# Two-layer hybrid encoder in exact-split fp32: rotary product and k's remainder from GpSimd to VectorE, softmax scaling from VectorE to ScalarE, three banks of transposes per head, and the per-layer input products inside the mixers

## Chip, cores and metric

One core of one Trainium2 chip. The metric is the device time of one launch in microseconds (us), the median of the runs. The five engines are named as the profile names them: PE is TensorE (PEld its weight loads), DVE VectorE, ACT ScalarE, POOL GpSimd, SP SyncE, which here only issues DMAs.

## What is computed

A residual stream h of 512 positions by 1024 features goes through two layers, in fp32:

```python
h = h + 0.5 * swiglu(rmsnorm(h, norm_ffn1[i]), ffn1_w_gate[i], ffn1_w_up[i], ffn1_w_down[i])
hn = rmsnorm(h, norm_mix[i])
if i % 2 == 0:
    h = h + ab_mixer(hn, w_in_ab[j], sink_a[j], w_out_ab[j], pos)
else:
    h = h + c_mixer(hn, w_in_c[j], rpb_c[j], w_out_c[j])
h = h + 0.5 * swiglu(rmsnorm(h, norm_ffn2[i]), ffn2_w_gate[i], ffn2_w_up[i], ffn2_w_down[i])
gate = jax.nn.sigmoid(rmsnorm(h, norm_ple[i]) @ w_ple_gate[i])
h = h + gate * (p[i] @ w_ple_proj[i])
```

and a last rmsnorm. The inner width of swiglu is 2816, p[i] has 256 features. The even layer's mixer has two parts on one projection. Part A is banded attention of 12 query heads on 4 key heads (|i-j| <= 128, rotary, a sink logit per head). Part B is dilated attention of 4 slots in three groups (offsets up to 64, 4 x 64 and 16 x 64), whose outputs are merged by their softmax denominators. The odd layer's mixer (part C below) is 16 heads of 8 x 16 neighbourhood attention with a position bias.

## The kernel before

**Layout.** Activations are held feature by position: eight chunks of 128 features by 512 positions. A product in full fp32 precision is made of three fp32r matmuls: each weight and each activation is split into a rounded part and the remainder (`split`, lines 120 to 122: ACT writes `hi`, another engine writes `lo = src - hi`), and `mm3` (lines 139 to 144) adds hi·hi, hi·lo and lo·hi. Weights come in units of 128 x 1024 (`unit`, line 129): SP issues the load, ACT makes `wh` (L121), DVE or POOL makes `wl` (L122). Three raw, four `wh` and four `wl` buffers are in turn. A wide matmul has 512 moving columns; the v projection (`project_v`, L322 to L324) has 256.

**Stages.** `setup`, then per layer `ffn`, `ab` or `c`, `ffn`, `ple`. In the trace `ab` is 376 to 660 us, `c` 1465 to 1700, the two `ple` about 1050 to 1106 and 2064 to 2125.

**Norm.** The norm's gain goes into the activation's split (`norm_split`); its factor per position comes late: `stat` (L187 to L190) makes `rcol`, one column per block of 128 positions, and `spread` transposes it into R, a row per position (property `R`, L206 and L214), by which products are scaled after the matmul.

**The AB mixer.** `ab` makes a list `steps` (scores and softmax, then p·v, head by head, from `a_steps` and `b_steps`) and a list `fill` (projections of q, k and v, then the first output products); `weave` (line 503) puts fill between steps by weights and by what a step needs. The order of each engine's own queue is then fixed by a scheduler before the run; `high_priority` marks pull some instructions ahead. Each engine runs its queue in order.

- `rope` (line 394) rotates a projected chunk: DVE shuffles (L404) and multiplies by the cosine (L405) out of PSUM, POOL multiplies by the sine (L406), DVE adds (L409, or L412 and L415 in another order of positions). It runs 20 times, 8 of them for part A.
- `stack_q` and `stack_k` (lines 262 to 285) write the rounded half and the remainder of a chunk. For k the remainder is made by POOL (L283), 8 times in `ab` and 16 times in `c`, and a DMA (L282) copies the rounded half to the other 64 partitions.
- `a_soft` (line 559), for each of 12 heads: four score blocks of 256 or 384 keys (`scores`, L428 on PE, L429 on DVE), ACT takes the exponentials with their sums (L568), DVE inverts the sums (L570) and scales the four blocks (L572).
- `windows_pv` (line 362) takes, for each of four key blocks, the two or three query blocks that see it, transposes them into one PSUM bank (`transposed`, L349), splits the bank on ACT and DVE (L121, L122) and multiplies by v (`pv`, L359 and L360). A's 12 heads and B's four slots do this: 16 times four banks.
- `b_steps`: `soft` for two slots, then `merge` (line 611), a chain of small DVE instructions (L617 to L634) that ends in the scaling of the blocks (L638), then `pv_r` (transposes L647, products L653) and `pv_n`.

**ple.** For each of eight output chunks, 24 wide matmuls of the gate and 6 of the product of p with `plp`, then DVE, ACT, DVE, DVE: the scaling by R, the sigmoid, the product, the sum. The last chunk of the last layer is done in two halves of positions. The two chunks of p are loaded and split at the stage's start.

## Time and profile before

| | us |
|---|---|
| runs: median of 3 (lowest to highest) | 2126.72 (2126.21 to 2127.21) |
| the profiled execution's own time | 2126.64 |
| its span in the trace | 2124.8 |
| PE busy in the span | 2085.4 |
| DVE busy | 1132.3 |
| ACT busy | 783.8 |
| POOL busy | 352.3 |

Read it so: PE is busy for all but 39.4 us of the span, so the other engines count only where PE stands idle for them, or where its clock is lowered. In the 40 slices of the page PE shows a digit under 9 only in the first and the last slice; the mixers' waits are too short for that view and are read from the waits of PE and from finer windows. Matmul ends are modelled, so a busy PE is not a PE at its peak.

### The profile page before, as it was taken

The page shows a single profiled execution, that of the slowest core. Times are in us where ns is not written, and L with a number is a line of the kernel's source. Part 1 is how long each engine was busy: PE and PEld are TensorE (multiplying, and loading weights), DVE is VectorE, ACT ScalarE, POOL GpSimd, SP SyncE. Part 2 cuts the span into 40 slices and gives each one's busy share as a digit, 9 for nine tenths or more (in the row PEclk, how much of TensorE's full clock was granted, in tenths as well). Part 3 has the DMA queues.
Part 4 walks back from the last instruction along what each step waited for, and adds up shares of the span by engine and source line. Part 5 has one row for each costly group of instructions (what it writes and reads, how often), then busy time and mean ns, then how long its engine had stood idle before and what let it go on. Part 6 is the DMA issues. An engine that isn't in the chain of part 4 may idle for free.

```text
span 2124.8 us, 25520 instructions
## 1 busy us (share of the span) xinstructions
PE 2085.4 (98%) x9950; PEld 1734.6 (82%) x9950; DVE 1132.3 (53%) x1793; ACT 783.8 (37%) x1255; POOL 352.3 (17%) x248
## 2 busy tenths in 40 slices
PE   8999999999999999999999999999999999999998
PEld 6888888777787888888888888888888888888886
DVE  6554432699786444543354555333778744553334
ACT  4332222465544333222343233223656533232232
POOL 3111101233211111101111111013222210110111
PEclk9999999999999999999999999999999999999999
DMA  5333333221223233333333322334333223323331
GB/s 171 98 99 99 95 96 98 85 75 56 65 68 92 90 99 99 99 90 96 105 97 99 99 93 93 95 97 124 105 105 102 82 90 99 99 91 96 94 107 60
DMA packets 75385, 202.02 MB, mean 95 GB/s; under 512 B 16896, under 2 KB 24576, under 8 KB 75264
## 3 DMA queue, kind: packets, MB, share of 16 engines
q1 hardware_dynamic: 74976, 200.29, 30.8%
q8 instruction: 78, 1.28, 0.3%
q14 instruction: 43, 0.35, 0.1%
q10 hardware_dynamic: 288, 0.10, 0.0%
HBM read 191.97 MB, written 2.59 MB: 92 GB/s over the span
## 4 chain that ended last, share of the span: by engine, by line
PE 89%; DVE 5%; ACT 2%; issue 1%; POOL 1%; DMA 0%; SPq 0%; DVEq 0%; POOLq 0%; ACTq 0%
PE mm L143 15%; PE mm L144 15%; PE mm L142 15%; PE sc L142 12%; PE sc L143 12%; PE sc L144 12%; PE mm L322 1%; PE mm L323 1%; PE mm L324 1%; PE tr L349 1%; PE ob L359 1%; PE ob L360 1%; PE sc L428 1%; ACT wh L121 1%; DVE act L572 1%
## 5 line engine op out<-in xcount | busy, mean ns | idle before, releaser
L121 ACT ACTIVATE wh<-wr 128x1024 fp32r<-128x1024 f32 (+1 forms) x360 | 374.6, 1042 | 995.0 <-issue 431.1
L122 DVE TENSOR_TENSOR wl<-wr,wh 128x1024 fp32r<-128x1024 f32 (+1 forms) x343 | 510.2, 1488 | 314.1 <-ACT wh L121 313.1
L143 PE MATMUL mm<-act,wh 128*128 128x512 f32 (+1 forms) x1560 | 609.7, 391 | 3.0 <-DVE act L169 2.1
L142 PE MATMUL mm<-act,wh 128*128 128x512 f32 (+1 forms) x1560 | 609.1, 391 | 1.0 <-ACT wh L121 0.6
L144 PE MATMUL mm<-act,wl 128*128 128x512 f32 (+1 forms) x1560 | 608.3, 390 | 0.5 <-DVE wl L122 0.5
L144 PE MATMUL sc<-act,wl 128*128 128x512 f32 (+1 forms) x1138 | 442.5, 389 | 0.8 <-DVE wl L122 0.8
L142 PE MATMUL sc<-act,wh 128*128 128x512 f32 (+1 forms) x1138 | 442.9, 389 | 0.0
L143 PE MATMUL sc<-act,wh 128*128 128x512 f32 (+1 forms) x1138 | 442.5, 389 | 0.0
L143 PEld LDWEIGHTS mm<-act,wh 128*128 128x128 f32 x1560 | 293.4, 188 | 64.4 <-DVE act L169 5.3
L142 PEld LDWEIGHTS mm<-act,wh 128*128 128x128 f32 x1560 | 293.3, 188 | 60.0 <-ACT act L121 1.5
L144 PEld LDWEIGHTS mm<-act,wl 128*128 128x128 f32 x1560 | 293.2, 188 | 58.4 <-DVE wl L122 1.0
L239 POOL TENSOR_TENSOR tmp<-tmp,tmp 128x512 f32<-128x512 f32 x88 | 115.2, 1309 | 818.5 <-DVE tmp L238 783.7
L144 PEld LDWEIGHTS sc<-act,wl 128*128 128x128 f32 x1138 | 213.7, 188 | 45.1 <-DVE wl L122 1.2
L143 PEld LDWEIGHTS sc<-act,wh 128*128 128x128 f32 x1138 | 213.7, 188 | 44.1
L142 PEld LDWEIGHTS sc<-act,wh 128*128 128x128 f32 x1138 | 213.6, 188 | 43.8
L238 DVE TENSOR_TENSOR tmp<-sc,R 128x512 f32<-128x512 f32 x88 | 60.8, 691 | 276.8 <-PE sc L144 276.8
L180 POOL TENSOR_TENSOR ssq<-ssq,tmp 128x512 f32<-128x512 f32 x55 | 90.2, 1639 | 552.6 <-ACT tmp L175 525.7
L236 DVE TENSOR_TENSOR tmp<-mm,R 128x512 f32<-128x512 f32 x88 | 60.8, 691 | 130.4 <-PE mm L144 127.9
L121 ACT ACTIVATE act<-tmp 128x512 fp32r<-128x512 f32 x92 | 58.3, 634 | 117.3 <-POOL tmp L239 116.2
L322 PE MATMUL mm<-wh,act 128*128 128x256 f32 x256 | 74.4, 291 | 0.3 <-DVE act L337 0.3
L323 PE MATMUL mm<-wl,act 128*128 128x256 f32 x256 | 73.9, 289 | 0.0
L324 PE MATMUL mm<-wh,act 128*128 128x256 f32 x256 | 73.8, 288 | 0.0
(142 smaller groups left out, 1621.8 us busy)
## 6 DMA issues: line engine op xcount, KB each, us to landing
wr<-in_gu_dram SPq DMA_DIRECT2D x176, 512.0 KB, 3.5
wr<-in_dn_dram SPq DMA_DIRECT2D x64, 512.0 KB, 3.5
wr<-in_dn_dram SPq DMA_DIRECT2D x32, 384.0 KB, 3.1
wr<-in_qk_ab_dram SPq DMA_DIRECT2D x20, 512.0 KB, 3.5
wr<-in_plg_dram SPq DMA_DIRECT2D x16, 512.0 KB, 3.5
wr<-in_qk_c_dram SPq DMA_DIRECT2D x16, 512.0 KB, 3.7
act<-act SPq DMA_DIRECT2D x40, 128.0 KB, 2.2
wr<-in_v_ab_dram SPq DMA_DIRECT2D x8, 512.0 KB, 3.8
```

Source lines behind the costliest of these rows:

```text
L121: self.nc.scalar.activation(hi, src, AF.Copy)
L122: (lo_eng or self.nc.vector).tensor_tensor(lo, src, hi.bitcast(F32), op=ALU.subtract)
L142: mm(out, stat[0], mov[0], start=start, stop=False)
L143: mm(out, stat[0], mov[1], start=False, stop=False)
L144: mm(out, stat[1], mov[0], start=False, stop=stop)
L180: eng.tensor_tensor(self.acc, self.acc, sq, op=ALU.add)
L236: nc.vector.tensor_tensor(t1, pgu[0], R, op=ALU.mult)
L238: nc.vector.tensor_tensor(t2, pgu[1], R, op=ALU.mult)
L239: nc.gpsimd.tensor_tensor(t2, t1, t2, op=ALU.mult)
L322: nc.tensor.matmul(ps[b], xh, h, start=first, stop=False, skip_group_check=True)
L323: nc.tensor.matmul(ps[b], xh, l, start=False, stop=False, skip_group_check=True)
L324: nc.tensor.matmul(ps[b], xl, h, start=False, stop=last, skip_group_check=True)
```

## The change

- `rope`: the product with the sine (new L435) is made by VectorE.
- `stack_k`: k's remainder (new L287) is made by VectorE, in both mixers.
- `a_soft`: ScalarE scales the blocks (new L613).
- `windows_pv`: three groups of key blocks, (1), (2) and (0, 3), with 384, 384 and 512 columns, in place of four banks of 256, 384, 384 and 256. The 10 transposes and the 8 products per head stay.
- `ple_proj`: the products of p[i] with `plp` (8 chunks of 6 wide matmuls per layer) become fill steps of `ab` and of `c`. ACT copies each from PSUM (L417), SP stores it in DRAM (L418), and `ple` loads it again (L888). In `ab` two of them stand near the start, six at the end; in `c` they come after the projections.
- The start of `ab`: the first k and q are projected before R is spread (`first`), and the first v, the second v (`vb`) and the rest change places in `fill`.
- `act` has 60 buffers, 59 before; `identb`, which nothing reads, is gone; `idle` takes R's buffer.

```diff
@@ spread, R
+    def spread(self, rcol, late=False):
...
-            self.nc.tensor.transpose(rp[:, b * P:(b + 1) * P], rcol[:, b:b + 1].broadcast_to([P, P]), self.ident)
+            ins = self.nc.tensor.transpose(rp[:, b * P:(b + 1) * P], rcol[:, b:b + 1].broadcast_to([P, P]), self.ident)
+            if late and b == 0:
+                self.tc.keep_in_program_order(ins)
@@ stack_k
-            nc.gpsimd.tensor_tensor(low[hf][own, :], k[own, :], t[own, :].bitcast(F32), op=ALU.subtract)
+            nc.vector.tensor_tensor(low[hf][own, :], k[own, :], t[own, :].bitcast(F32), op=ALU.subtract)
@@ windows_pv
+    GROUPS = ((1,), (2,), (0, 3))
...
+        for g in self.GROUPS:
+            at = [(x, b) for x in g for b in range(*self.window(x))]
+            off = lambda x, b: (x - self.window(b)[0]) * P
+            parts = self.transposed([es[b][:, off(x, b):off(x, b) + P] for x, b in at])
+            n = 0
+            for x in g:
+                lo, hi = self.window(x)
+                m = n + (hi - lo) * P
+                self.pv(o[:, lo * P:hi * P], vcol(x), [y[:, n:m] for y in parts], g == (1,), x == 3)
+                n = m
@@ new
+    def ple_proj(self, i):
+        nc, io = self.nc, self.io
+        c = {"p": []}
+        for k in range(2):
+            raw = self.tmp()
+            nc.sync.dma_start(raw, io["pT"][i, :, k, :])
+            c["p"].append(self.split_chunk(raw, nc.vector))
+        def chunk(m):
+            if m % 4 == 0:
+                c["u"] = self.unit(io["plp"][i, m // 4])
+            s = m % 4 * 2 * P
+            b = self.sbank() if i == 0 and m < 2 else self.bank()
+            self.mm_unit(b, tuple(x[:, s:s + 2 * P] for x in c["u"]), c["p"], True, True)
+            t = self.tmp()
+            nc.scalar.activation(t, b, AF.Copy)
+            nc.sync.dma_start(self.pp[i, m], t)
+        return [(("pp", m), .25, lambda m=m: chunk(m)) for m in range(KC)]
@@ rope
-        nc.gpsimd.tensor_tensor(t2, t2, self.sinr, op=ALU.mult)
+        nc.vector.tensor_tensor(t2, t2, self.sinr, op=ALU.mult)
@@ ab
+        def first():
+            pk = self.project(w[12])
+            self.rcol
+            pq = self.project(w[13])
+            self.spread_R(late=True)
+            end_k(0, pk)
+            end_q(0, 0, pq)
...
-        fill = (a0[:2] + proj_v("va", 0) + a0[2:] + a1 + proj_b(0) + proj_v("vb", 1) + proj_v(("vr", 0), 2)
-                + proj_b(1) + proj_v(("vr", 1), 3))
+        b0, b1, pp = proj_b(0), proj_b(1), self.ple_proj(0)
+        fill = (a0[:1] + pp[:2] + proj_v("va", 0) + a0[1:] + proj_v("vb", 1) + a1 + b0
+                + proj_v(("vr", 0), 2) + b1 + proj_v(("vr", 1), 3) + pp[2:])
@@ a_soft
-            nc.vector.tensor_scalar_mul(es[b], es[b], rd[:, b:b + 1])
+            nc.scalar.activation(es[b], es[b], AF.Copy, scale=rd[:, b:b + 1])
@@ c
+        fill += self.ple_proj(1)
@@ ple
+            pm = self.tmp()
+            nc.sync.dma_start(pm, self.pp[i, m])
...
-                pg, pp = self.bank()[:, x], self.sbank()[:, x]
+                pg = (self.sbank() if m % 2 else self.bank())[:, x]
                 self.mm_unit(pg, u, cut(xg), True, True)
-                self.mm_unit(pp, upm, cut(p), True, True)
...
-                nc.vector.tensor_tensor(t2, pp, t1, op=ALU.mult)
+                nc.vector.tensor_tensor(t2, pm[:, x], t1, op=ALU.mult)
```

How this moves instructions, at three places. The number behind a tile's name tells one buffer of that name from another.

**The start of `ab`, on TensorE.** `mm_2622` (after: `mm_2603`) is the first q's projection, `tr_2589` (after: `tr_2629`) the transposes that spread R, `mm_2731` the first v's projection. Before:

```order
L142 MATMUL mm_2622<-act_2062,wh_2617 128x512
L143 MATMUL mm_2622<-act_2063,wh_2617 128x512
L144 MATMUL mm_2622<-act_2062,wl_2618 128x512
L206 MATMUL tr_2589<-ident,rcol_2586 128x128 x4
L142 MATMUL mm_2622<-act_2155,wh_2617 128x512
L143 MATMUL mm_2622<-act_2156,wh_2617 128x512
```

After:

```order
L141 MATMUL mm_2603<-act_2526,wh_2598 128x512
L142 MATMUL mm_2603<-act_2527,wh_2598 128x512
L143 MATMUL mm_2603<-act_2526,wl_2599 128x512
L206 MATMUL tr_2629<-ident,rcol_2594 128x128 x4
L326 MATMUL mm_2731<-wh_2734,act_1876 128x256
L327 MATMUL mm_2731<-wl_2735,act_1876 128x256
```

The four transposes stood behind 9 of the 24 matmuls of that projection and stand behind all 24 now. From them to the first scores there were 15 wide matmuls and 39 of 256 columns; now there are 95 of 256 columns.

**Part A's softmax.** The second head's scaling and the first head's split banks (`tmp<-tr`), before on VectorE:

```order
L122 TENSOR_TENSOR tmp_2900<-tr_2896,tmp_2899 128x256
L569 TENSOR_TENSOR st_a_2816<-st_a_2816 128x4
L409 TENSOR_TENSOR act_2886<-tmp_2881,tmp_2882 128x512
L570 RECIPROCAL st_a_2816<-st_a_2816 128x4
L122 TENSOR_TENSOR tmp_2910<-tr_2905,tmp_2909 128x384
L572 TENSOR_SCALAR act_2818<-act_2818,st_a_2816 128x256
L572 TENSOR_SCALAR act_2823<-act_2823,st_a_2816 128x384
L122 TENSOR_TENSOR tmp_2920<-tr_2915,tmp_2919 128x384
L572 TENSOR_SCALAR act_2828<-act_2828,st_a_2816 128x384
L122 TENSOR_TENSOR tmp_2929<-tr_2925,tmp_2928 128x256
L572 TENSOR_SCALAR act_2833<-act_2833,st_a_2816 128x256
```

After, on ScalarE (L609 is the exponential, L613 the scaling):

```order
L613 ACTIVATE act_2688<-act_2688,st_a_2671 128x256
L609 ACTIVATE act_2855,st_a_2853<-act_2855,st_a_2853 128x256
L120 ACTIVATE tmp_2937<-tr_2933 128x384
L607 ACTIVATE st_a_2853<-st_a_2853 128x4
L609 ACTIVATE act_2860,st_a_2853<-act_2860,st_a_2853 128x384
L120 ACTIVATE tmp_2947<-tr_2943 128x384
L609 ACTIVATE act_2865,st_a_2853<-act_2865,st_a_2853 128x384
L609 ACTIVATE act_2870,st_a_2853<-act_2870,st_a_2853 128x256
L120 ACTIVATE tmp_2958<-tr_2953 128x512
L613 ACTIVATE act_2855<-act_2855,st_a_2853 128x256
```

The scalings left VectorE's queue and stand in ScalarE's behind the next head's exponentials and the split of the bank before.

**The first merge of part B, on VectorE.** Before:

```order
L617 COPY s_b_4591<-st_b_4240 32x4 x16
L621 TENSOR_TENSOR zs_b_4610<-s_b_4591,st_b_4240 128x8
L622 TENSOR_TENSOR w_b_4608<-s_b_4591,zs_b_4610 128x2x4
L623 TENSOR_TENSOR w_b_4608<-st_b_4240,zs_b_4610 128x2x4
L625 TENSOR_TENSOR z_b_4609<-w_b_4608,s_b_4591 128x2x4
L626 TENSOR_TENSOR z_b_4609<-w_b_4608,st_b_4240 128x2x4
L627 TENSOR_TENSOR zs_b_4610<-z_b_4609 128x8
L628 RECIPROCAL zs_b_4610<-zs_b_4610 128x8
L629 TENSOR_TENSOR w_b_4608<-w_b_4608,zs_b_4610 128x2x4
L630 TENSOR_TENSOR w_b_4608<-w_b_4608,zs_b_4610 128x2x4
L634 COPY w_b_4621<-w_b_4608 32x2 x16
L638 TENSOR_SCALAR act_4263<-act_4263,w_b_4608 128x256
```

After, its first and its last rows (the copies are L658 and L675 now, the scaling L679):

```order
L433 STREAM_SHUFFLE tmp_4663<-mm_4637 128x512
L434 TENSOR_TENSOR tmp_4662<-mm_4637,act_2635 128x512
L658 COPY s_b_4568<-st_b_4339 32x4 x12
L435 TENSOR_TENSOR tmp_4663<-tmp_4663,act_2636 128x512
L658 COPY s_b_4568<-st_b_4339 32x4 x4
L662 TENSOR_TENSOR zs_b_4587<-s_b_4568,st_b_4339 128x8
L438 TENSOR_TENSOR act_4667<-tmp_4662,tmp_4663 128x512
```

```order
L675 COPY w_b_4598<-w_b_4585 32x2 x6
L433 STREAM_SHUFFLE tmp_4713<-mm_4687 128x512
L434 TENSOR_TENSOR tmp_4712<-mm_4687,act_2635 128x512
L675 COPY w_b_4598<-w_b_4585 32x2 x10
L679 TENSOR_SCALAR act_4362<-act_4362,w_b_4585 128x256
```

Six instructions of two rotations (L433, L434, L435, L438, L433, L434) stand inside the chain now; before there were none between its first copy and its first scaling. On TensorE, between the last score product ahead of this merge and the first transposition behind it, there were 29 matmuls of 256 columns and 25 wide ones, and there are 46 wide ones now. At the second merge there were 25 and 28, and there are 24 and 26; its chain on VectorE has no rotation in it, before or after.

## Rows read from the trace of the kernel before

**Rows 1.** The page's first part: an engine's busy time, its share of the span, its instructions.

```profile
PE 2085.4 (98%) x9950; PEld 1734.6 (82%) x9950; DVE 1132.3 (53%) x1793; ACT 783.8 (37%) x1255; POOL 352.3 (17%) x248
```

**Rows 2.** Busy time by stretch: start and end in us; its length; then, for PE, PEld, DVE, ACT and POOL, the busy us and the number of instructions; then the granted clock of PE, the DMA share and GB/s. The four stretches of `ab` (its start, part A, the first and the second half of part B), an `ffn`, and `c`.

```profile
376.00:397.00 21.00, 17.02 (x98) 14.86 (x97) 12.25 (x20) 5.27 (x8) 10.81 (x8) 0.95 0.39 124
397.00:545.00 148.00, 140.00 (x804) 118.24 (x803) 129.14 (x330) 87.82 (x212) 43.42 (x31) 1.00 0.20 61
545.00:600.00 55.00, 51.12 (x278) 42.09 (x277) 41.41 (x119) 25.23 (x61) 15.79 (x11) 0.91 0.21 63
600.00:660.00 60.00, 57.05 (x357) 47.45 (x356) 43.29 (x128) 27.25 (x67) 2.57 (x2) 1.00 0.16 54
660.00:1040.00 380.00, 380.00 (x1684) 314.77 (x1683) 175.97 (x169) 118.53 (x147) 51.67 (x35) 1.00 0.32 100
1465.00:1700.00 235.00, 230.27 (x1365) 200.36 (x1365) 169.09 (x447) 135.20 (x282) 63.13 (x42) 1.00 0.35 101
```

**Rows 3.** The waits of PE over the whole span: which instruction waited for which; us in total, times, longest. The row behind the dots is from the same view of part A alone (397 to 545 us), since it waits so in other stages too.

```profile
PE tr L349 <- DVE act L572: 5.1, 6, 1.6
PE tr L647 <- DVE act L638: 4.3, 2, 2.6
PE sc L428 <- DVE act L270: 2.5, 1, 2.5
PE tr L206 <- POOL rcol L190: 1.4, 1, 1.4
...
PE ob L360 <- DVE tmp L122: 2.4, 2, 1.6
```

**Rows 4.** Busy time by stretch, as in rows 2, for the three stretches of `ab` in which PE's granted clock was 0.50.

```profile
394.80:398.20 3.40, 2.93 (x11) 2.93 (x12) 2.28 (x7) 0.06 (x1) 0.00 (x0) 0.50 0.03 11
548.40:555.20 6.80, 6.24 (x25) 5.70 (x25) 3.71 (x15) 6.05 (x21) 0.00 (x0) 0.50 0.00 0
568.90:572.30 3.40, 2.94 (x8) 2.46 (x9) 3.37 (x8) 0.00 (x0) 1.89 (x3) 0.50 0.15 48
```

**Rows 5.** The chain that ended last, followed through the start of `ab`: start us, us, engine, tile and line.

```profile
380.53 2.39 POOL wl L122
...
383.96 0.67 PE tr L206 x4
...
384.65 0.61 ACT R L214
...
386.65 1.29 POOL tmp L406
...
391.78 1.78 DVE act L409
...
394.24 0.98 DVE act L270
395.23 0.04 issue
395.27 0.80 PE sc L428 x2
```

**Rows 6.** Groups of equal instructions of the AB mixer (376 to 660 us), shapes kept apart: line, engine, operation, tiles, shapes, count; busy us in all, mean ns of one; idle us before them and what ended it.

```profile
L406 POOL TENSOR_TENSOR tmp<-tmp,act 128x512 f32<-128x512 f32 x20 | 25.7, 1293 | 78.5 <-DVE tmp L404 65.2 <-PE mm L324 6.7 <-ACT wh L121 3.4
...
L572 DVE TENSOR_SCALAR act<-act,st_a 128x256 f32<-128x256 f32 x24 | 16.5, 687 | 0.2
...
L404 DVE STREAM_SHUFFLE tmp<-mm 128x512 f32<-128x512 f32 x20 | 15.0, 748 | 0.0
...
L283 POOL TENSOR_TENSOR act<-act,act 64x512 fp32r<-64x512 f32 x8 | 13.8, 1722 | 9.0 <-ACT act L281 8.8
L405 DVE TENSOR_TENSOR tmp<-mm,act 128x512 f32<-128x512 f32 x20 | 13.5, 676 | 0.1
...
L572 DVE TENSOR_SCALAR act<-act,st_a 128x384 f32<-128x384 f32 x24 | 9.4, 418 | 0.0
...
L331 ACT ACTIVATE act<-mm,rcol 128x256 f32<-128x256 f32 x8 | 3.2, 469 | 0.0
...
L401 DVE TENSOR_TENSOR act<-act,R 128x512 f32<-128x512 f32 x1 | 0.7, 684 | 0.0
```

**Rows 7.** VectorE and then POOL in order of time around 439 us: start us, us, engine, line, operation, tiles, shapes, count (equal ones merged), in brackets the idle time before. The last row is the view of L572 alone: shortest, median and longest of one in ns, the first's and last's start.

```profile
438.87 2.99 DVE L572 TENSOR_SCALAR act<-act,st_a 128x256 f32<-128x256 f32 x4
...
438.42 2.37 POOL L122 TENSOR_TENSOR wl<-wr,wh 128x1024 fp32r<-128x1024 f32 x1 [9.95 <-ACT wh L121]
...
L572 DVE TENSOR_SCALAR act<-act,st_a x48: 336/407/2480, 404.4 to 537.1; 128x256 f32<-128x256 f32 x24, 128x384 f32<-128x384 f32 x24
```

**Rows 8.** Two matmuls of the v projection that follow each other, in order of time.

```profile
388.73 0.28 PE L323 MATMUL mm<-wl,act 128*128 128x256 f32 x1
388.85 0.28 PE L324 MATMUL mm<-wh,act 128*128 128x256 f32 x1
```

**Rows 9.** Around the first merge, in order of time: TensorE behind the last score product and at the first transposition, then ScalarE, then VectorE.

```profile
557.30 0.39 PE L323 MATMUL mm<-wl,act 128*128 128x256 f32 x1
...
569.36 0.47 PE L647 MATMUL tr<-ident,act 128*128 128x128 f32 x1 [2.62 <-DVE act L638]
...
558.20 1.06 ACT L121 ACTIVATE wh<-wr 128x1024 fp32r<-128x1024 f32 x1 [3.25 <-PE mm L324]
...
559.79 4.63 DVE L617 COPY s_b<-st_b 32x4 f32<-32x4 f32 x16 [1.39 <-ACT act L608]
```

**Rows 10.** VectorE at the very end, in order of time: the last scalings by gain and norm.

```profile
2116.20 5.17 DVE L917 SCALAR_TENSOR_TENSOR act<-h,gain,tr 128x256 f32<-128x256 f32 x13
```

More of the change, by code (lines that the diff above doesn't have):

```diff
@@ L60, in __init__ @@
         self.open = {}
+        self.pp = self.dp.tile([DEPTH, KC, P, T], F32, name="pp")
     def nm(self, s):
@@ L104, in setup @@
         nc.scalar.activation(warm, self.ones[:, 0:1], AF.Silu)
-        idle = self.cp.tile([P, T], BF16, name="idle")
+        idle = self.small("R", [P, T], BF16, bufs=1)
         nc.vector.memset(idle, 0.0)
@@ L210, in R, with spread_R @@
     def R(self):
-        if self.rt is None:
-            self.rt = self.small("R", [P, T], bufs=1)
-            self.nc.scalar.activation(self.rt, self.spread(self.rcol), AF.Copy)
+        return self.rt or self.spread_R()
+    def spread_R(self, late=False):
+        self.rt = self.small("R", [P, T], bufs=1)
+        self.nc.scalar.activation(self.rt, self.spread(self.rcol, late), AF.Copy)
         return self.rt
@@ L459, in proj, with end_k, end_q @@
             return key, 1, lambda: t.__setitem__(key, self.rope(self.project(w[i]), kind))
-        def proj_a(gp):
-            def k_step():
-                k, low = self.rope(self.project(w[12 + 4 * gp]), "n"), self.lows()
-                t["ak", gp] = (self.stack_k(k, low), low)
-            def q_step(j):
-                t["aq", gp, j] = self.stack_q(self.rope(self.project(w[13 + 4 * gp + j]), "n"))
-            return [(("ak", gp), 1, k_step)] + [(("aq", gp, j), 1, lambda j=j: q_step(j)) for j in range(3)]
+        def end_k(gp, p):
+            k, low = self.rope(p, "n"), self.lows()
+            t["ak", gp] = (self.stack_k(k, low), low)
+        def end_q(gp, j, p):
+            t["aq", gp, j] = self.stack_q(self.rope(p, "n"))
+        def first():
[5 more added lines that the diff above has]
+            end_q(0, 0, pq)
+        def proj_a(gp):
+            out = [(("aq", gp, j), 1, lambda j=j: end_q(gp, j, self.project(w[13 + 4 * gp + j]))) for j in range(1 - gp, 3)]
+            k = ("ak", 1), 1, lambda: end_k(1, self.project(w[16]))
+            return [k, *out] if gp else [(("ak", 0), 2, first), *out]
         def proj_b(sp):
@@ L553, in a_steps @@
             if i < len(heads):
-                steps.append(([("ak", gp), ("aq", gp, heads[i][1])], 1, lambda h=heads[i]: soft(*h)))
+                need = [("ak", gp)] + [("aq", gp, heads[i][1])] * (gp + heads[i][1] > 0)
+                steps.append((need, 1, lambda h=heads[i]: soft(*h)))
             if i:
@@ L841, in ple @@
         nc, io = self.nc, self.io
-        xg, p = self.xg, []
-        for c in range(2):
-            raw = self.tmp()
-            nc.sync.dma_start(raw, io["pT"][i, :, c, :])
-            p.append(self.split_chunk(raw))
-        up, ends = None, []
+        xg, ends = self.xg, []
         for m in range(KC):
             u = self.unit(io["plg"][i, m])
-            if m % 4 == 0:
-                up = self.unit(io["plp"][i, m // 4])
-            s = m % 4 * 2 * P
-            upm = tuple(x[:, s:s + 2 * P] for x in up)
+            pm = self.tmp()
+            nc.sync.dma_start(pm, self.pp[i, m])
             half = k_next == N_NORM - 1 and m == KC - 1
```

13 lines of the change are left out of this document (1 added, 12 removed).

## The prediction, made before the changed kernel ran

> **What bounds the kernel now.** The page's first part comes first: PE is busy 2085.4 of a span of 2124.8 us [rows 1], so all that can be won is 39.4 us of idle PE and the stretches in which its clock is lowered. The profiled execution took 2126.64 us, 1.84 more than its span and 0.08 under the median of the runs, 2126.72. My sum is made against 2126.64. The table by stretch comes next: an `ffn` has no idle PE, and of the AB mixer its start has 4.0 us (21.00 less 17.02), part A 8.0, the two halves of part B 3.9 and 2.95, the mixer of the second layer 4.7 [rows 2]. The change touches the mixers and `ple` alone. The waits of PE then say whom these gaps wait for: VectorE's scaling in A (5.1), the merges (4.3), the first scores (2.5), R (1.4), and in A VectorE's split of a bank (2.4) [rows 3]. Last, the clock: the granted clock is 0.50 (1.2 GHz of 2.4) in three stretches around such gaps, with 2.93, 6.24 and 2.94 us of matmuls in them [rows 4]. Half of each, 1.5, 3.1 and 1.5 us, is what full clock would give back.
>
> TensorE's own work does not change. 48 wide matmuls per layer move from `ple` to the mixer, each 0.226 us (380.00 over 1684 [rows 2]); a v-projection matmul starts 0.12 us behind the last [rows 8]. A move in itself is worth nothing, except where a moved matmul stands where PE waited.
>
> **Start of `ab`: -4.9.** Before, R's transposes run at 383.96 after a wait of 1.4, R is written at 384.65, and the rotation and k's split end at 395.23, when PE has long run out [rows 3, 5]. In the changed order 15 more wide matmuls, 3.4 us, stand ahead of the transposes, more than the 1.4 waited: that wait goes. Behind them stand 95 half-width matmuls, 11.4 us. PE is free at 382.56 without its wait, begins R at 386.0, ends it (0.67) at 386.6 and arrives at the scores at 398.0. The chain: R to 387.3 (0.61), cosine and sine by R (2 x 0.68 [rows 6]), two rotations begun (0.68, 0.75, 0.68, 2 x 0.68, 0.69), a weight's split that waits for a free buffer and then takes 1.06 [rows 9] and a subtraction of two times 0.68, then the remainders, sum and copies: about 398.1. The two nearly meet, so 2.0 of the 2.5 goes, and with it the low-clock stretch, 1.5. Bounds: -5.4 if the whole wait goes, -1.4 if R's alone does.
>
> **Part A: -4.8.** Here the trace says why VectorE is late. The 128x256 scaling takes 687 ns on average, the wider 128x384 one 418 [rows 6]; four small ones take 2.99 us where POOL makes a `wl` of 2.37 at the same time, and of all 48 the shortest takes 336 and the longest 2480 [rows 7]. So one that meets POOL's subtraction stands still for it. On VectorE over the whole mixer: 20 sine products of two SBUF inputs at 0.684 (the row L401), +13.7; 8 remainders, +5.5; two `plp` units and two chunks of p split, +2.7 and +1.4; the scalings, -16.5 and -9.4 [rows 6]. That is 2.6 less in 284 us, and PE no longer waits for it between exponential and transpose. ScalarE gets 24 scalings at about 0.47 (L331, the same shape) and 24 at about 0.6, an estimate from it by the columns: some 25 us, so in A its 87.8 of 148 busy [rows 2] becomes some 113 of the 143 left, 79%. POOL loses 25.7 and 13.8. I take all of the 5.1, half of the 2.4, and give 1.5 back for heads whose scaling stands behind other work of ScalarE, since the first transposition now needs three scaled blocks, not two. Bounds: -7.5 (both waits gone) to +6.4 (a rival below).
>
> The three groups in place of four banks spare 16 instructions on each of ScalarE and VectorE. They have no price of their own here and lie under PE's work; counted at nothing.
>
> **First merge: +2.4.** The last score product starts at 557.30, the first transposition at 569.36 after a wait of 2.62, and the 16 small copies at 559.79 after 1.39 idle [rows 9]. Six instructions of rotations now stand inside this chain: 0.75 + 0.68 + 0.68 + 0.69 + 0.75 + 0.68, 4.2 us by the rows of L404, L405 and L401 [rows 6]. The first two fit in the 1.39 idle, so the chain grows from 12.1 to 14.9. PE's cover grows too, from 9.44 to 46 x 0.226 = 10.4. The wait becomes 4.5, +1.9, and I add 0.5 for a longer stretch at low clock. Bounds: 0 (the rotations are done before the chain can begin) to +4.8 (nothing fits in the idle time, +1.4, and one more stretch like the third of [rows 4], +1.5).
>
> **Second merge: +0.9.** Its chain stays; its cover falls by one half-width and two wide matmuls, 0.6 us, more if the low clock holds on: 0 to +2.
>
> **The mixer of the second layer: -0.6.** 16 remainders go from POOL, 1722 ns each [rows 6], to VectorE at 0.684, 11 us in a stage where VectorE is busy 169.09 of 235 [rows 2], and the 48 moved products give cover at its end. Bounds -2 to +2: its 4.7 us of gaps have many owners.
>
> **`ple` and the end: -0.7.** Each of the 16 chunks is now stored and loaded again. The load stands on SP behind the weights' loads; the work that hides it is 24 matmuls of the gate (5.4 us) and the sigmoid. If it is late, only the sum of h is late, and the other weights of the gate go on: counted at nothing within `ple`. At the very end six half-width matmuls (6 x 0.12) no longer stand between the last two halves; VectorE's 5.17 us of last scalings [rows 10] may hide them all, so -0.7 to 0.
>
> **Sum:** -4.9 - 4.8 + 2.4 + 0.9 - 0.6 - 0.7 = -7.7, so 2118.9. The longest low-clock stretch, in A's last heads (6.24 us), I leave as it is, since p·v and scores alternate there as before.
>
> **The rivals.** A measurement tells about 0.2%, 4.3 us, from no change: below 2122.4 is faster, above 2130.9 slower.
>
> *ScalarE becomes what A waits for: slower (0.10).* Each of 12 heads' scalings may stand behind one weight split, 1.06 [rows 9]: 12.7 in place of the waits, A +6.4. It decides once a head waits for over 0.6 us on average (that is 7.5 over 12). With the merge at its upper bound: -4.9 + 6.4 + 4.8 + 0.9 - 0.6 - 0.7 = +5.9, 2132.5. For it: the queue is in order and A is already ScalarE's fullest stretch of `ab`. Against: 79% is not full, and splits are made ahead of need.
>
> *VectorE is not relieved: no change (0.18).* In A the waits only change name (A 0), and the merge comes at its upper bound: -0.5, 2126.1. The rows allow it: undisturbed, the scalings cost 24 x 0.336 + 24 x 0.407 [rows 7], 17.9 us and not 25.9, against 23.3 us added. VectorE then has 5.4 us more to do, and if POOL's subtraction no longer meets anything it stops, nothing is won by moving. With the merge as forecast this gives -4.9 + 0 + 2.4 + 0.9 - 0.6 - 0.7 = -2.9, 2123.7; 0.08 of the 0.18 is this one. The Trainium skill, "VectorE: DVE Perf Modes", section "Mode 2×_2P — use both read ports for one tensor", speaks for it: a scaling of one fp32 tensor can use both read ports and make two results per cycle, while a product of two tensors cannot, so the change trades VectorE's cheap kind of work for its dear one. The trace agrees on the rates (from 336 ns, the shortest, which has 256 columns, to 407, about what 384 take, 128 columns cost 71 ns, while 512 columns of two tensors take 684); but the four scalings of 2.99 us show that the cheap rate was not had where it counted, and I follow them.
>
> *Relief carries through: faster by more (0.17).* The waits of A all go, the chain of the merge is reached early, and the low-clock stretch of A's last heads goes too: -5.4 - 7.5 + 0 - 3.1 + 0.9 - 0.6 - 0.7 = -16.4, 2110.2. Against: the rotations stand inside the chain by VectorE's order.
>
> That the moved products do not fill what waited is already in the sum: they get 0.6 at most.
>
> **How the numbers follow.** The forecast has 0.55; its own range is 2114 to 2124 (the bounds of start, A's share of 2.4 and merge taken together but not all at one end), 0.05 of it above 2122.4. Faster: 0.50 + 0.17 = 0.67. Same: 0.05 + 0.18, less 0.02 for its worst part: 0.21. Slower: 0.12. The range from 2110.0 to 2128.0 leaves out half of the larger gain (0.085) and the slower cases (0.11).
>
> **What would show it.** Start: no wait for `rcol`, a wait under 1 us for the first scores, full clock at 394.8. A: the waits of the transposes name ScalarE's scaling, and add up to under 3 us. Merge: a wait of about 4.5 before the first transposition and rotations between the small copies. End: less idle PE. I am wrong if the waits for scalings in A exceed 6 us, if the first merge waits for under 2.5 or over 6, or if a wait appears in `ple` for the loaded products.

## The result, and the profile after

The changed kernel takes 2130.26 us (median of 17 runs, 2127.36 to 2133.48) against 2126.22 of the kernel before in the same comparison: ratio 1.0019, 95% interval 1.0011 to 1.0026. That is 4 us slower, where 7.7 us faster were forecast. The profiled execution took 2133.08, 2.8 over its median, with a span of 2131.3, so the stretches below hold some 2.8 us that a usual run does not have.

The page's first line answers to [rows 1]:

```profile
PE 2089.5 (98%) x9944; PEld 1735.0 (81%) x9944; DVE 1132.7 (53%) x1776; ACT 808.7 (38%) x1303; POOL 285.6 (13%) x200
```

The stretches of [rows 2, 4], with the same columns; the last four are the low-clock stretches of the AB mixer:

```profile
376.00:397.00 21.00, 19.22 (x113) 17.40 (x112) 11.49 (x19) 5.22 (x8) 5.38 (x4) 0.92 0.41 136
397.00:545.00 148.00, 140.12 (x758) 115.47 (x757) 115.96 (x276) 105.56 (x246) 21.90 (x14) 0.97 0.22 66
545.00:600.00 55.00, 49.48 (x302) 41.53 (x301) 46.15 (x136) 28.62 (x66) 7.37 (x5) 0.97 0.20 63
600.00:660.00 60.00, 56.64 (x353) 46.52 (x352) 44.61 (x127) 28.25 (x67) 0.00 (x0) 1.00 0.30 97
1465.00:1700.00 235.00, 232.33 (x1377) 202.16 (x1377) 170.91 (x464) 138.65 (x291) 35.80 (x25) 1.00 0.39 115
...
392.20:395.61 3.41, 3.41 (x19) 3.41 (x18) 1.88 (x4) 0.00 (x0) 0.00 (x0) 0.50 0.05 22
457.05:463.88 6.83, 5.53 (x13) 4.42 (x14) 4.97 (x13) 5.73 (x17) 0.00 (x0) 0.50 0.25 77
480.94:484.36 3.42, 3.42 (x11) 2.90 (x11) 1.93 (x10) 1.78 (x6) 0.00 (x0) 0.50 0.22 86
579.93:583.34 3.41, 3.34 (x10) 2.77 (x11) 3.41 (x14) 0.00 (x0) 0.00 (x0) 0.50 0.00 0
```

The relief came: in part A VectorE is busy 115.96 and not 129.14, GpSimd half as long, ScalarE 105.56 [rows 2]. But PE does 140.12 in those 148 us, no more than before, and part A now has two low-clock stretches of its own. The waits of PE name others than before [rows 3]:

```profile
PE tr L688 <- DVE act L679: 5.7, 2, 4.1
PE sc L457 <- DVE st_a L458: 3.5, 3, 1.9
PE tr L206 <- POOL rcol L189: 3.5, 2, 1.7
PE ob L364 <- DVE tmp L121: 3.0, 4, 1.4
PE ob L363 <- ACT tmp L120: 2.8, 11, 0.4
PE tr L206 <- POOL rcol L940: 2.4, 2, 1.3
...
PE mm L141 <- DVE tmp L434: 1.9, 1, 1.9
PE mm L326 <- DVE tmp L434: 1.8, 1, 1.8
```

No transposition of part A waits for a scaling any more. Scores wait for VectorE (L458), products for a split bank (L364, L363), a projection for a rotation to read its bank (L434). And two waits of 1.7 us for R's factor stand in `ple`, where there were none.

The table says where the time went. From each stretch's length I take its matmuls, each at the time from one start to the next of its kind at full clock (0.2265 us wide, 0.176, 0.12 and 0.11 for 384, 256 and 128 columns), so that the moved products cancel; what is left is waiting and low clock, in us. "Products back" (the products of p in `ple` again) and "four, late" (four banks and a later R in `ple`) are two of the experiments below.

| stretch, to | before | after | products back | four, late |
|---|---|---|---|---|
| `ab`'s first scores (from the first `ffn`'s R) | 4.8 | 4.4 | 0.9 | 4.4 |
| part A's last score | 17.0 | 20.4 | 22.0 | 11.5 |
| first merge's transposition | 9.0 | 6.2 | 6.5 | 6.9 |
| second merge's | 7.4 | 9.1 | 9.3 | 9.8 |
| R of the next `ffn` | 3.1 | 4.0 | 5.8 | 3.5 |
| R of `ple`, both | 1.1 | 4.4 | 1.1 | 0.7 |
| R of the `ffn` after `ple` | 0.5 | 1.4 | 0.5 | 0.4 |
| through the second mixer to the next `ffn`'s R | 11.3 | 8.4 | 11.0 | 8.6 |
| from the last `ple`'s R to the end | 11.0 | 13.4 | 11.1 | 13.1 |

The column after is 6.5 above before, the difference of the two spans. Its largest losses are part A +3.4, `ple`'s R +3.3 and the end +2.4. The kernel with the late R below has the same order of instructions on every engine up to `ple`; in its profile part A loses 2.5 and the start is 1.9 below before, so the first two rows differ by 1.0 and 1.5 from one execution to another.

### The profile page after: what moved, and what is told of

It is laid out like the page before. It is cut to its first block, busy times and chain, and to the rows that moved or that the text cites. A ratio compares the mean times of both kernels' runs of the same rounds, so it can differ in the third digit from the quotient of the medians.

```text
span 2131.3 us, 25531 instructions
## 1 busy us (share of the span) xinstructions
PE 2089.5 (98%) x9944; PEld 1735.0 (81%) x9944; DVE 1132.7 (53%) x1776; ACT 808.7 (38%) x1303; POOL 285.6 (13%) x200
## 4 chain that ended last, share of the span: by engine, by line
PE 69%; DVE 4%; issue 3%; ACT 3%; DMA 1%; POOL 0%; DVEq 0%; SPq 0%; ACTq 0%; POOLq 0%
PE mm L141 12%; PE mm L142 12%; PE mm L143 11%; PE sc L143 9%; PE sc L141 9%; PE sc L142 9%; PE mm L328 1%; PE mm L327 1%; PE mm L326 1%; PE ob L363 1%; PE tr L353 1%; ACT wh L120 1%; PE ob L364 1%; PE sc L457 1%; PE sc L840 0%
## 5 line engine op out<-in xcount | busy, mean ns | idle before, releaser
L141 PE MATMUL mm<-act,wh 128*128 128x512 f32 x1516 | 596.3, 393 | 3.0 <-DVE tmp L434 1.9
L142 PE MATMUL mm<-act,wh 128*128 128x512 f32 x1516 | 595.0, 392 | 2.3 <-DVE act L168 2.2
L143 PE MATMUL mm<-act,wl 128*128 128x512 f32 x1516 | 594.7, 392 | 0.5 <-DVE wl L121 0.5
L143 PE MATMUL sc<-act,wl 128*128 128x512 f32 (+1 forms) x1180 | 457.7, 388 | 0.8 <-DVE wl L121 0.8
L141 PE MATMUL sc<-act,wh 128*128 128x512 f32 (+1 forms) x1180 | 457.8, 388 | 0.0
L142 PE MATMUL sc<-act,wh 128*128 128x512 f32 (+1 forms) x1180 | 457.6, 388 | 0.0
L142 PEld LDWEIGHTS mm<-act,wh 128*128 128x128 f32 x1516 | 285.9, 189 | 61.9 <-DVE act L168 5.8
L141 PEld LDWEIGHTS mm<-act,wh 128*128 128x128 f32 x1516 | 286.3, 189 | 60.6 <-DVE tmp L434 2.1
L143 PEld LDWEIGHTS mm<-act,wl 128*128 128x128 f32 x1516 | 286.0, 189 | 57.3 <-DVE wl L121 1.0
L143 PEld LDWEIGHTS sc<-act,wl 128*128 128x128 f32 x1180 | 221.6, 188 | 46.5 <-DVE wl L121 1.2
L142 PEld LDWEIGHTS sc<-act,wh 128*128 128x128 f32 x1180 | 221.7, 188 | 45.4
L141 PEld LDWEIGHTS sc<-act,wh 128*128 128x128 f32 x1180 | 221.5, 188 | 45.1
L121 POOL TENSOR_TENSOR wl<-wr,wh 128x1024 fp32r<-128x1024 f32 x17 | 41.4, 2435 | 253.0 <-ACT wh L120 253.0
```

Of the source, the lines that this page charges most:

```text
L121: (lo_eng or self.nc.vector).tensor_tensor(lo, src, hi.bitcast(F32), op=ALU.subtract)
L141: mm(out, stat[0], mov[0], start=start, stop=False)
L142: mm(out, stat[0], mov[1], start=False, stop=False)
L143: mm(out, stat[1], mov[0], start=False, stop=stop)
```

## Experiments

Each ratio is taken against runs of the kernel before on the same chip. A difference of 0.001 is 2.1 us; where two intervals overlap, no difference is shown by the times alone.

**The late R.** R's transposes stand later in `ple`.

```diff
                 if m == 0:
-                    R = self.R
...
+                if m == 1:
+                    for q in range(KC):
+                        self.mm3(pg, us[q], xg[q], q == 0, q == KC - 1)
+                        if q == 3:
+                            R = self.spread_R(late=True)
```

> The changed kernel, with the transposes that spread R in ple standing behind 12 wide matmuls from the statistics (4 of the 8 input chunks of the second output chunk), where they stand behind 2; nothing else is changed. Theory P (the gate's start lost its cover when the products of p went to the mixers): the two waits for rcol L189 in ple, 2.4 us in all, and the weight-load idle around them go; 3.3 to 4 us less than the changed kernel's 2130.3, so about 2126.6. Rival M (all of the loss is in the mixers): the wait moves to VectorE, which now scales the first chunk later, and the time stays within 1 us of 2130.3.

Measured 2125.47, ratio 0.9999 (0.9990 to 1.0008): 4.8 us below the changed kernel. Theory P holds, with a little more than its 3.3 to 4 us, and no transposition waits for L189 any more (its 2.4 us were misread: that is the row of L940 at the end; L189 has 3.5). TensorE in the first `ple`, in order of time, before and then after:

```profile
1051.17 0.95 PE L187 MATMUL tr<-ones,ssq 128*128 128x1 f32 x8
...
1053.47 0.65 PE L206 MATMUL tr<-ident,rcol 128*128 128x128 f32 x4
```

```profile
1063.53 0.95 PE L186 MATMUL tr<-ones,ssq 128*128 128x1 f32 x8
1064.34 0.47 PE L141 MATMUL sc<-act,wh 128*128 128x512 f32 x1
1064.65 0.40 PE L142 MATMUL sc<-act,wh 128*128 128x512 f32 x1
...
1066.79 0.65 PE L206 MATMUL tr<-ident,rcol 128*128 128x128 f32 x4 [1.74 <-POOL rcol L189]
```

Between the statistics (`ones,ssq`) and the transposes there stood five matmuls of the gate and there are two. The chain is also longer: GpSimd's 128x4 power, which makes `rcol`, took 1.02 us there before and takes 1.98 now, next to a weight subtraction of VectorE of 1.23. Before, then after:

```profile
1052.40 1.02 POOL L190 TENSOR_TENSOR rcol<-ms,mhalf 128x4 f32<-128x4 f32 x1 [1.87 <-DVE ms L189]
```

```profile
1064.63 1.23 DVE L121 TENSOR_TENSOR wl<-wr,wh 128x1024 fp32r<-128x1024 f32 x1
...
1064.75 1.98 POOL L189 TENSOR_TENSOR rcol<-ms,mhalf 128x4 f32<-128x4 f32 x1 [17.48 <-DVE ms L188]
```

So about 1.0 of the 1.74 us is the longer power, and 0.7 the three matmuls that are missing.

**Single parts undone in the changed kernel.** One line is changed in each.

```diff
-            nc.scalar.activation(es[b], es[b], AF.Copy, scale=rd[:, b:b + 1])
+            nc.vector.tensor_scalar_mul(es[b], es[b], rd[:, b:b + 1])
-        nc.vector.tensor_tensor(t2, t2, self.sinr, op=ALU.mult)
+        nc.gpsimd.tensor_tensor(t2, t2, self.sinr, op=ALU.mult)
-            nc.vector.tensor_tensor(low[hf][own, :], ...)
+            nc.gpsimd.tensor_tensor(low[hf][own, :], ...)
```

> The changed kernel, with part A's scaling of the blocks back on VectorE. Theory Q (the scaling on ScalarE only moved the wait: four scalings, 1.93 us in a row, stand in front of the split of the next bank, VectorE waits for that and TensorE for VectorE): 2 to 4 us faster than 2130.3. Rival R (the scaling's move is the part that gains, and the sine product and remainder on VectorE use it up): 4 to 8 us slower, waits of transposes for the scaling come back with over 5 us in all.

Measured 2131.92, 1.0030 (1.0018 to 1.0042); the interval overlaps the changed kernel's. Rival R's waits of the transposes for the scaling came back with 4.0 in part A, but not its time.

> The changed kernel, with the sine product of the 20 rotations back on GpSimd. Theory Q (VectorE's queue holds the rotation's read of PSUM behind other work, and TensorE waits for the bank): 2 to 4 us faster than 2130.3, no wait of a projection for L434 and a shorter wait at the first merge (4.1 to about 2.6). Rival R (GpSimd's products hold VectorE still whenever both read SBUF, so the product is cheaper on VectorE): 3 to 6 us slower; instructions of VectorE next to GpSimd's product take more than twice their usual time.

Measured 2131.59, 1.0024 (1.0015 to 1.0033): no difference that can be told. The first merge's wait is 5.0 there, not shorter, so the sine product's engine is not what makes it long.

> The changed kernel, with k's remainder back on GpSimd, in both mixers. Theory Q: the wait of the scores for VectorE in part A (2.02 us at 480 us, behind a remainder of 2.40 us) goes, and in the second layer's mixer nothing changes: 1 to 3 us faster than 2130.3. Rival R: the second mixer's gain (its gaps were 2.9 us fewer in the profile of the changed kernel than before) goes back: 2 to 4 us slower, all of it between 1465 and 1720 us.

Measured 2141.46, 1.0075 (1.0063 to 1.0088): 11 us slower, far beyond either theory; the waits of products for VectorE's split bank grew from 3.0 to 6.5, and its profile loses 1 to 2 us in each of the start, part A, both merges, the second mixer and the end. Undoing any one of the three moves between engines makes the kernel slower or no different, so none of them alone is the loss.

**Groups, start and products undone.**

```diff
-        for g in self.GROUPS:
+        for x in range(NB):
...
-            pk = self.project(w[12])
-            self.rcol
-            pq = self.project(w[13])
-            self.spread_R(late=True)
...
+        fill = (a0[:2] + proj_v("va", 0) + a0[2:] + a1 + b0 + proj_v("vb", 1) + proj_v(("vr", 0), 2)
+                + b1 + proj_v(("vr", 1), 3) + pp)
...
-        fill += self.ple_proj(1)
...
+                self.mm_unit(pp, upm, cut(p), True, True)
```

> The changed kernel, with the four banks of 256, 384, 384 and 256 columns per head in place of the three groups. Theory G (the groups are what loses in part A: the first transposition needs three scaled blocks, and the last bank of 512 columns is split and multiplied in one piece, so each head's last products wait longer): 3 to 6 us faster than 2130.3, most of it between the first score and the first merge. Rival H (the groups save 16 instructions on ScalarE and VectorE each and lose nothing): 1 to 3 us slower.

Measured 2125.93 (before 2124.82 here), 1.0008 (0.9999 to 1.0016): 0.0011 or 2.3 us below the changed kernel, less than the 3 to 6 of Theory G, and the intervals overlap. Part A's stretch fell from 20.4 to 13.1, where Theory G put the gain; some of it is lost again behind (the second merge's stretch is 1.8 longer).

> The changed kernel, with the first k and q, R and the order of the v projections as before; all eight products of p stand at the end of the mixer's fill. Theory S (the late R, with rotations and the second v ahead of part A's other projections, is what loses in part A): 2 to 5 us faster than 2130.3, although the wait of 1.6 for R and the wait of the first scores come back. Rival T (the new start is a gain): 2 to 4 us slower, nearly all of it before the first scores.

Measured 2132.42, 1.0033 (1.0021 to 1.0046): 3 us more by the ratios, but the interval overlaps the changed kernel's. Theory S's gain is not there. The profiled execution, the fastest of its five (a span of 2126.7), shows no loss ahead of the scores, so Rival T is not shown either.

> The changed kernel, with the products of p back in ple and no copies or stores of them in the mixers. Theory P: R's waits in ple go (2.4 us and what follows them) and the tail is shorter, since the products stand again between the last halves; about 6 us faster than 2130.3 (4.8 by the run with the late R, and 1 to 2 at the tail), so about 2124, if the mixers don't need the products as cover. Rival U (the products are what covers the second layer's mixer and the merges): the second layer's mixer goes back by 2.9 us, the time is within 2.5 us of 2130.3.

Measured 2129.84, 1.0025 (1.0015 to 1.0035): rival U. The table's third column shows both sides: `ple` and the end are as before again (6.5 us better than after), while the second mixer lost 2.6, the stretch behind the second merge 1.8 and part A 1.6. The start gained 3.5. One reason for that lies in the helper that gives every third unit's remainder to GpSimd (line 125): with the units of `plp` gone from the mixer, other weights fall to GpSimd, and at 386.80 us VectorE makes a remainder where GpSimd makes one at 386.90 in the changed kernel. What that one costs is shown below.

**Two parts alone on the kernel before.**

```diff
-            nc.gpsimd.tensor_tensor(low[hf][own, :], ...)
+            nc.vector.tensor_tensor(low[hf][own, :], ...)
...
-        for x in range(NB):
+        for g in self.GROUPS:
```

> The kernel before, with k's remainder on VectorE in both mixers and nothing else changed. Theory K (this move is a gain by itself, since the remainder waits on GpSimd behind weight splits of 2.4 us; putting it back cost the changed kernel 11 us): 4 to 10 us faster than 2126.2. Rival L (it gains only where VectorE has been relieved of the scaling and GpSimd of the sine product): within 2 us of 2126.2, with longer waits of the transposes for the scaling.

Measured 2133.82, 1.0043 (1.0030 to 1.0055): 9 us slower, against both theories. Part A's stretch holds 8 of them: the waits for the scaling are no longer than before (4.8), but scores wait there 4.6 us for VectorE to read the scores before them (L429; 0.2 before). The same move that is worth 11 us in the changed kernel costs 9 in the kernel before.

> The kernel before, with the three groups of key blocks per head and nothing else changed. Theory G1 (the groups cost by themselves: the first transposition needs three scaled blocks and the last bank is split in one piece of 512 columns): 3 to 7 us slower than before, with the waits of the transposes for the scaling up from 5.1. Theory G2 (they cost only where ScalarE does the scaling and so stands ahead of the next bank's split): within 1.5 us of before.

Measured 2134.15, 1.0039 (1.0027 to 1.0052): 8 us slower. The groups cost by themselves: G1, slightly beyond its range (waits for the scaling 4.0, though, not more than 5.1; 2.5 for L433, the scores' reading, came in addition). Part A's stretch has 3.3 of the loss and the first merge's 2.3; part B's slots use the groups too.

**Why the groups cost.** First the long split, then the third block.

```diff
+            for x in (slice(0, n // 2), slice(n // 2, n)) if halve else (slice(0, n),):
+                self.split(t[:, x], hi[:, x], lo[:, x])
```

> The changed kernel, with the third group's bank of 512 columns split in two pieces of 256, one per key block; transposes, banks and order of the groups stay. Theory G3 (the long split of the last bank is what makes each head late): back to the ratio of the four banks, 1.0008, about 2.4 us faster than the changed kernel. Theory G4 (it is that the first group needs three blocks, and the last bank four): no gain, 1.0019 to 1.0025, since ScalarE and VectorE only get 16 instructions more each.

Measured 2131.72, 1.0028 (1.0016 to 1.0040): no gain, about as Theory G4 expected. This does not clear the long split altogether: the run's profile has a part A that is 5.3 shorter than that of the changed kernel, and the stretches behind it are longer.

> The changed kernel with two edits: four banks per head as before, and R's transposes in ple behind 12 matmuls. If the two losses are independent, their ratios add (0.9999 and 1.0008 against the changed kernel's 1.0019): 0.9988, some 2.5 us faster than the kernel before. If the groups' cost lay only in how the order fell out, the sum need not hold: 0.998 to 1.001.

Measured 2120.46 (before 2126.17), 0.9975 (0.9966 to 0.9985): faster than both kernels, and by more than the sum of the two. Beside the late R, then, the groups cost 5 us (0.9999 less 0.9975). This kernel with its four banks in another order:

```diff
-        for x in range(NB):
+        for x in (1, 2, 0, 3):
```

> The kernel of the last study that had four banks and the late R (0.9975), with its four banks in the order of the key blocks 1, 2, 0, 3, so that the first transposition needs three scaled blocks, as with the groups. Theory G4 (it is the third block that each head waits for): most of the groups' cost comes back, 0.999 to 1.001. Theory G5 (it is three banks in place of four: two of the banks are in turn, and the third, larger one can begin only when the first is split): stays within 0.001 of 0.9975.

Measured 2129.51 (before 2126.3), 1.0019 (1.0010 to 1.0028). Theory G4, beyond its range: with four banks as before, beginning with one that needs the third block gives back 9 us. (That first bank also has 384 columns in place of 256; the run does not tell the two apart.) The waits of PE in part A, first of the kernel with four banks and late R, then of this one:

```profile
PE sc L453 <- DVE st_a L454: 1.6, 2, 1.1
PE mm L141 <- DVE tmp L430: 0.8, 1, 0.8
PE ob L363 <- ACT tmp L120: 0.8, 1, 0.8
PE ob L364 <- DVE tmp L121: 0.5, 2, 0.3
```

```profile
PE sc L453 <- DVE st_a L454: 2.8, 3, 1.9
PE tr L353 <- ACT act L609: 1.8, 3, 1.1
PE ob L364 <- DVE tmp L121: 1.5, 3, 1.2
PE sc L453 <- issue: 0.8, 1, 0.8
```

The late first bank shows up as waits of transpositions (L353) for a scaling (L609 here), which the first kernel does not have, and as longer waits of products (L364) and of the next scores (L453). That these follow from it, through the order of the queues, is argued. Where the first kernel keeps full clock through part A (granted clock 1.00 from 397 to 545), the second falls to 0.98.

> The kernel with four banks and the late R, with part A's scaling back on VectorE. The prediction's term for part A (the scaling on ScalarE takes the waits of the transposes away) would show here without the groups: waits of transposes for the scaling come back with 3 to 5 us, and the time is 4 to 6 us more, 0.9995 to 1.0005. Rival (the scaling's move is worth as little as beside the groups, 1.0030 against 1.0019): 0.998 to 0.999.

Measured 2128.95, 1.0015 (1.0006 to 1.0024): 8.5 us slower, more than the 4 to 6 expected; the transpositions wait 5.3 us for the scaling again. Without the groups the scaling's move to ScalarE is worth that much.

**GpSimd beside VectorE, and the end.**

```diff
-        return self.nc.vector if self.turn else self.nc.gpsimd
+        return self.nc.vector if self.turn or self.k == 1 else self.nc.gpsimd
...
-            eng = nc.vector if c == KC - 1 and self.k else nc.gpsimd
+            eng = nc.vector if c == KC - 1 and self.k or c == KC - 2 and self.k == N_NORM - 1 else nc.gpsimd
```

> The changed kernel, with the nine remainders of weights that GpSimd makes in the first layer's mixer (2.4 us each) made by VectorE (1.2 us each). Theory H (an instruction of VectorE that reads and writes SBUF alone stands still while GpSimd subtracts): the instructions of VectorE of 2 us and more in that stretch, 8.5 us over their usual times in all, go, VectorE's busy time there grows by 11 less 6 to 8 us, the wait of 2.0 for the scores at 480 us goes; the time is 1 to 3 us less than 2130.3. Rival (they come from VectorE's own queue and stay): VectorE is busy 11 us longer and the time is 2 to 5 us more.

Measured 2134.27, 1.0039 (1.0025 to 1.0052): the long instructions go as Theory H says, the time is as the rival says, though its interval just touches the changed kernel's. VectorE and GpSimd at the mixer's start and at 477 us, after:

```profile
387.34 2.51 DVE L429 TENSOR_TENSOR act<-act,R 128x512 f32<-128x512 f32 x1 [4.66 <-ACT R L218]
389.78 0.68 DVE L430 TENSOR_TENSOR act<-act,R 128x512 f32<-128x512 f32 x1
...
477.04 2.40 DVE L274 TENSOR_TENSOR act<-act,act 64x512 fp32r<-64x512 f32 x1
...
386.90 2.40 POOL L121 TENSOR_TENSOR wl<-wr,wh 128x1024 fp32r<-128x1024 f32 x1 [3.94 <-ACT wh L120]
...
476.50 2.38 POOL L121 TENSOR_TENSOR wl<-wr,wh 128x1024 fp32r<-128x1024 f32 x1 [21.98 <-ACT wh L120]
```

and the same product, and all of L274 in the mixer (shortest, median, longest), with the nine remainders on VectorE:

```profile
388.06 0.69 DVE L429 TENSOR_TENSOR act<-act,R 128x512 f32<-128x512 f32 x1
...
L274 DVE TENSOR_TENSOR act<-act,act x16: 684/685/689, 398.2 to 592.6; 64x512 fp32r<-64x512 f32 x16
```

The longest L274 fell from 2395 to 689 ns, and the stretch up to the first scores from 4.4 to 0.9 us. The wait at 480 us is gone too. But part A's stretch grew by 3.0: one wait of scores for VectorE is 3.7 us long there and ends at 451.6 us, and 17 us of low clock in one piece begin at 451.

> The kernel with four banks and the late R, with the seventh chunk's sum of squares ahead of the last norm on VectorE in place of GpSimd. Theory E (the products of p covered this sum between the last chunks; now the statistics of the last halves wait for it and all behind them comes later): the wait of 1.0 for ssq L179 at the end goes, and 0.9 to 1.5 us of the tail with it, about 0.9970. Rival (the end is set by the second half's chain through VectorE alone): no change of over 0.3 us at the tail.

Measured 2119.59, 0.9970 (0.9959 to 0.9982); the end's stretch fell from 13.1 to 12.2, as Theory E says. The wait in question, in the last 70 us of the kernel with four banks and late R, then of this one:

```profile
PE tr L947 <- POOL ssq L179: 1.0, 1, 1.0
```

```profile
PE tr L947 <- DVE ssq L179: 0.2, 1, 0.2
```

It covers 0.9 of the 2 us that the end lost. The 0.9 cannot be told in the medians; the two kernels' intervals overlap.

## Why the prediction was wrong

**Part A, -4.8: the step that failed.** The prediction wrote of the groups that they spare 16 instructions and are "counted at nothing", and gave 1.5 us back for heads that wait, "since the first transposition now needs three scaled blocks, not two", a figure worked out from no row. The stretch became 3.4 longer (2.5 in the profile of the late R), so the term missed by 7 to 8 us. Without the groups the rest of it holds: the stretch falls from 17.0 to 11.5 (-5.5 against -4.8), and the scaling's move is worth 8.5. The groups cost 2.3 us in the changed kernel, by ratios whose intervals overlap, 5 beside the late R and 8 in the kernel before; beginning four banks with the third block costs 9. All four comparisons go the same way, and their size depends on what else stands in the queues. By the reordered run, the price is that each head's first bank is late, which goes on to the next scores and to the clock. In the changed kernel's own profile no transposition waits for a scaling; there the scores wait for VectorE. So how the groups' cost divides between the third block, the width of the banks and the order into which the scheduler puts the rest is not shown.

**`ple`, "counted at nothing": the second.** The prediction looked at the load of the products (VectorE waited 0.8 us for one, once; PE for none) and not at the statistics' chain to R. Beside that chain stood five matmuls, two stand there now, at both layers, and GpSimd's power takes 1.0 longer. R's two stretches lost 3.3 us, the one behind 0.9; the late R takes back 4.8. None of the five is a product of p, whose six stood just ahead of the statistics. But with the products back, five stand there again, the power takes 1.02 and the stretches are as before; why the scheduler leaves fewer without them is not shown.

With both undone the kernel is 5.7 us faster than before, where 7.7 were forecast and the changed kernel is 4.0 slower: the two steps hold 9.7 of the 11.7 us of the miss.

**The end, -0.7: the sign.** The products between the last halves were cover: with them back the end is as before. Measured +2.4, of which 0.9 is the last sum of squares. Another 1.4 stands in the waits for the last halves' factor: L940 has 2.4 us in two waits now, and before it was

```profile
PE tr L206 <- POOL rcol L906: 1.0, 1, 1.0
```

No run takes that wait away by itself.

**Start, -4.9: half failed.** R's wait went (waiting and low clock up to R's transposes fell from 2.0 to 0.4), and the first scores no longer wait. But the product with R's cosine stood still beside GpSimd's weight subtraction (2.51 in place of 0.68), so the v projection waited 1.8 for the rotation's bank and the clock fell at 392 instead of 395. The profile of the late R has the same wait and no low clock there, so that part is a matter of the execution. The profile of before had this mechanism in [rows 7], for scalings of one tensor; I did not carry it to products of two SBUF tensors. With that subtraction on VectorE the stretch falls to 0.9, 3.9 below before.

**First merge, +2.4: right in its mechanism.** The wait is 4.1 (forecast 4.5), and the rotations stand between the copies:

```profile
567.99 0.74 DVE L433 STREAM_SHUFFLE tmp<-mm 128x512 f32<-128x512 f32 x1
568.62 0.68 DVE L434 TENSOR_TENSOR tmp<-mm,act 128x512 f32<-128x512 f32 x1
569.21 2.09 DVE L658 COPY s_b<-st_b 32x4 f32<-32x4 f32 x12
571.31 0.69 DVE L435 TENSOR_TENSOR tmp<-tmp,act 128x512 f32<-128x512 f32 x1
572.01 0.70 DVE L658 COPY s_b<-st_b 32x4 f32<-32x4 f32 x4
```

The stretch still became 2.8 shorter: the low clock of 548 to 555 us [rows 4], which I left as it was, is gone from it (3.1), and so are three short waits (1.2 in all), against 1.5 more of this wait. **Second merge, +0.9:** +1.7, within its bounds.

**Second mixer, -0.6:** -2.9, beyond its bound of -2. Without the moved products 2.6 of it are lost again, which the prediction priced at 0.6 at most; with k's remainder back on GpSimd it is 1.7, so the two overlap.

**The rivals.** The measured +4.0 is nearest to "ScalarE becomes what A waits for" (+5.9), but by luck: no transposition waits for a scaling, and with the scaling back on VectorE the kernel is not faster. "VectorE is not relieved" gave the band of no change, in which the result lies, and its mechanism is wrong as well: from 376 us to the next `ffn`'s R, VectorE's busy time fell from 248.6 to 243.2 us. Its rates hold: the sine products and remainders cost what two-source work costs (0.77 and 0.68 us), and the scalings had been cheap where undisturbed.

```profile
L435 DVE TENSOR_TENSOR tmp<-tmp,act 128x512 f32<-128x512 f32 x20 | 15.2, 770 | 0.0
...
L613 ACT ACTIVATE act<-act,st_a 128x384 f32<-128x384 f32 x24 | 13.3, 602 | 0.0
...
L613 ACT ACTIVATE act<-act,st_a 128x256 f32<-128x256 f32 x24 | 12.0, 499 | 1.1 <-DVE st_a L611 0.8
...
L287 DVE TENSOR_TENSOR act<-act,act 64x512 fp32r<-64x512 f32 x8 | 5.5, 683 | 0.1
```

ScalarE's 25.3 us were forecast as some 25, and its scalings did not become what part A waits for.

None of the three signs that the prediction named for being wrong came: the waits for scalings are 0, the first merge waits 4.1, and PE waits for no loaded product. They watched the waits that were priced; most of the time was lost through terms that were counted at nothing.

What stays open: why k's remainder alone costs 9 us in the kernel before, whether the old start is slower at all, and how the groups' cost divides.

## What to carry to other kernels

Work that is moved away was cover for something: before pricing a move, count on the waiting engine's queue what is left between each producer chain and its consumer at the old place. A cheaper form of a pipeline stage (fewer, larger banks) may be paid for at its first piece: count how many inputs that piece needs, and try the order by itself, as the run with the banks 1, 2, 0, 3 did. And try the parts of a bundle both alone and taken out of it: k's remainder costs 9 us alone and is worth 11 in the bundle.

## What the runs showed of the hardware

**VectorE and GpSimd stand still for each other.** In the AB mixer 20 instructions of VectorE before and 9 after took over 0.25 us more than their kind's usual time, 19 and 10 us in all. Every one lay beside an instruction of GpSimd, and none read PSUM. The hold ends with GpSimd's instruction: six of the nine have 512 columns and usually take 0.68 to 0.69 us, and each of the six ended 0.55 us after the GpSimd instruction beside it (the product of 387.34 us at 389.85, GpSimd at 389.30). It works the other way as well (GpSimd's power 1.02, and 1.98 beside VectorE's subtraction). The Trainium skill, "GPSIMD Engine Reference", section "Specifications", says that GpSimd shares its SBUF interfaces with VectorE and contends with VectorE's two-port modes and with instructions of two SBUF inputs; the trace agrees for both kinds, [rows 7] for the first and L429 for the second.

**The spread goes with the clock.** The 17 runs of the changed kernel spread over 6.1 us, those of before over 2.5. Their mean granted clock goes from 0.996 at 2127.4 us to 0.993 at 2133.5. Gaps of PE of about 2 us in the mixer were followed by stretches at a granted clock of 0.50 (1.2 GHz), which one execution has and another has not: the late R's kernel, the same up to `ple`, had none at the start although PE waited the same 1.8 us there, and reached part A's last score 2.5 us sooner than the profile of the changed one.
